# Decode attention's index tables moved to the top of the kernel

## The chip, the cores and the metric

The kernel runs on one core of a Trainium2 chip. The metric is device time in microseconds (us) of one execution. Before the change, three runs took 1286.26, 1288.38 and 1287.98 us; the median is 1287.98 us.

A core has five engines with a queue each: PE (TensorE, matrix products and transposes), DVE (VectorE), ACT (ScalarE), POOL (GpSimd) and SP, which here only issues transfers. Each works through its queue in order and waits on semaphores set by the others. Transfers are issued by SP, ACT or POOL and are carried out by 16 DMA engines.

## The reference

One inference step of a two-layer decoder trunk on 512 new prompt tokens and on 8 decode sequences of 4 new tokens each, all in float32, with a model width of 1024. Layer 0 mixes tokens with a convolution module, layer 1 with stick-breaking attention (16 heads of 64), and each is followed by a gated feed-forward network with a short convolution (ConvFFN, width 2816). The decode sequences attend to 256 past tokens, which lie in a paged pool of 128-token pages:

```python
k_past = [jnp.take(cache_k[a], page_table, axis=0).reshape(db, past_len, N_HEADS, HEAD_DIM) ...]
z = jnp.einsum('bqhd,bkhd->bhqk', q, k) * (HEAD_DIM ** -0.5)
z = z + bias[None, :, None, None]
log_fail = jnp.where(valid, jax.nn.log_sigmoid(-z), 0.0)
after = lax.cumsum(log_fail, axis=3, reverse=True) - log_fail
weights = jnp.where(valid, jnp.exp(jax.nn.log_sigmoid(z) + after), 0.0)
```

`page_table` (8 sequences by 2 pages, int32) says which page of the pool holds which part of a sequence. `bias` is one learned number per head, and `valid` is the causal mask.

## The kernel before

Activations are kept transposed, 128 features on the partitions and 544 tokens (512 prompt, 32 decode) along the row, in eight blocks: xT is the residual stream, XH and XL are its normalised value split into a high and a low part. Each weight block (`raw`, 1 MB, two buffers) is loaded by `Ring.load` (L338), cast to a high part by ACT (L375, `whi`) and subtracted to a low part by DVE (L378, `wlo`). Every product is three matrix multiplications. The first twelve blocks (`CONV_RAWS`) are loaded through POOL's queue, except for the very first, which are loaded in halves on SP's (L349); the rest go through SP's.

The work is written as lists. A `Plan` takes operations with an engine, an estimated cost in us and the keys that they read and write. `Plan.run` simulates the engines and fixes the order in which operations are emitted: on each engine it takes the ready operation with the earliest start, less a small share of its rank (the longest chain of work behind it). Within a list the order on each engine stays as planned; operations that are emitted outside a list are mixed in by the compiler's own scheduler. There is one list for the convolution, one for each layer's ConvFFN (the function `ffn`) and one for the attention. The list of the first ConvFFN, here the first layer's list, also holds the query products of layer 1 (`queries`), and at its end the first steps of the decode attention.

Those steps are three. First, xT is saved to memory (L1801), for the space of xT is wanted for pages: `page_t` is three buffers of 128 tokens by 1024 over the front of xT. Second, `decode_tables` makes the small tables in thirteen pieces, each entered in the list as a DVE operation of 0.5 us that comes after `ready`, the point at which the second half's normalisation may begin. Third, `gather` (L1940) fetches the first three pages of K rows on POOL's queue, with row numbers from the table `idx`; they come after the save and after the tables. The remaining 13 K gathers and 16 V gathers belong to the attention's list and reuse the same buffers.

The tables are: `idx`, for each partition and page the row number in the pool (page number times 128 plus the partition); `bcol`, the head's bias on each partition; `mnew`, the mask among the new tokens; and `own`, which partition belongs to which sequence. They come from two counting patterns of POOL (`iota`, L1948 and L1950), from `page_table` broadcast to all partitions (L1952) and from the biases `bb`, likewise broadcast (L1750).

Between the two lists stand operations that belong to none: Qz (in xT) and Qf are cleared (L2016, L2017), queries of the decode tokens are copied into them on POOL (L2026, L2032), and ACT's function table is changed. The attention's list then begins with the key products (L2108 to L2110), which also serve as filling, and with `page_logits`: PE transposes one page in two halves into the single PSUM buffer `t` (L2216), DVE copies out the first half and ACT the second (L2220), and then logits are computed (L2228).

At the top of the kernel SP loads the first prompt rows and weights, while POOL clears a few tiles and issues 23 small loads of parameters (`prow`, L627 to L633, and `trow`, L638) ahead of its first weight block. DVE has little to do before the first rows of x arrive (L943).

Of the kernel before, what the change touches and what calls it, by code (L numbers as in the profile page):

```python
# [21 lines left out]
NB = 8  # L22
NI = 4
NS = NB * NI
# [5 lines left out]
H = 16  # L30
HD = 64
EPS = 1e-6
NEG = -1.0e30
# [9 lines left out]
MORE = 3  # L43
CONV_RAWS = 12
PLAINQ = 4
TABLES = 13

PASSES = ((0, 4), (4, 6), (10, 6), (16, 6))
FFN_CHUNKS = 6
# [178 lines left out]
def tile_trunk(  # L228
# [8 lines left out]
    nc = tc.nc  # L237
# [11 lines left out]
    def close(cm):  # L249
        cm.__exit__(None, None, None)  # L250
# [155 lines left out]
    xT = base.tile([P, NC, T], F32, name="xT")  # L406
    XH = base.tile([P, NC, T], F32R, name="XH")
    XL = base.tile([P, NC, T], F32R, name="XL")
    NPRM = 42
    prm = base.tile([P, NC, NPRM], F32, name="prm")  # L410
    fprm = base.tile([P, NF, 40], F32, name="fprm")
# [197 lines left out]
    trow = [start.tile([8 * n_g, P], F32, name=f"trow{i}") for i in range(2)]  # L609
    zero = conv.tile([P, 2 * P], BF16, name="zero")  # L610
    dve.memset(zero, 0.0)
    act.dma_start(out=mrow[2:4, :], in_=conv_b_in.rearrange("o (t d) -> (o t) d", t=2))
    act_table("sqrt_and_others")
    nc.sync.dma_start(out=mrow[0:2, :], in_=norm_mix)
# [19 lines left out]
    for i in range(2):  # L634
        ch0 = (PE_CHUNKS[0] + i * len(PE_CHUNKS) // 2) * P
        for m in range(8):
            nj = min(4, CW - 4 * m)
            pool.dma_start(out=trow[i][m * n_g:(m + 1) * n_g, :nj * 32].rearrange("g (j h) -> g j h", j=nj),  # L638
                          in_=conv_w_dw[0, 4 * m:4 * m + nj, ch0:ch0 + n_g * 32].rearrange("j (g h) -> g j h", h=32))


    plan = Plan(E_CONV, 0.12)
# [580 lines left out]
    def ffn(l, before, after):  # L1223
# [455 lines left out]
        def queries(s):  # L1679
# [61 lines left out]
            def kept():  # L1741
                close(pools["more_cm"])
                close(cm)
                att["qk_cm"], qk = open_pool("qk")
                att["qT"] = qk.tile([P, NC, T], F32, name="qT")
                att["kT"] = qk.tile([P, NC, T], F32, name="kT")
                att["bb"] = qk.tile([P, H], F32, name="bb")
                att["kT_s"] = qk.tile([P, NC, NS], F32, name="kT_s")
                att["dz_cm"], att["dz"] = open_pool("dz")
                nc.sync.dma_start(out=att["bb"], in_=attn_b_logit[0].partition_broadcast(P))  # L1750

            ready = plan.op("none", 0.0, kept, after=range(opened, len(plan.ops)))

# [45 lines left out]
                s += 4  # L1799
            xs = [("x", c, h) for c in range(NC) for h in range(2)]  # L1800
            plan.op("sp", 5.0, lambda: nc.sync.dma_start(out=xsave, in_=xflat), r=[*xs, "normed1"], w=["saved"])  # L1801
            tables = decode_tables()
            for _ in range(TABLES):
                plan.op("dve", 0.5, lambda: next(tables), w=["tables"], after=[ready])
            for j in range(PAGE_BUFS):
                plan.op("pool", 1.05, lambda j=j: gather(page_t[j], j, ck), r=["saved", "tables"])
            return s
# [32 lines left out]
        after = after()  # L1840
# [97 lines left out]

    def gather(t, j, src):
        pool.indirect_dma_start(out=t, out_offset=None, in_=src,  # L1940
                                in_offset=bass.IndirectOffsetOnAxis(ap=att["idx"][:, j:j + 1], axis=0))

    def decode_tables():
        dz = att["dz"]
        bb = att["bb"]
        small_cm, small = open_pool("dsmall")
        pid = small.tile([P, 1], I32, name="pid")
        pool.iota(pid, pattern=[[0, 1]], base=0, channel_multiplier=1)  # L1948
        t32 = small.tile([P, NS], I32, name="t32")
        pool.iota(t32, pattern=[[1, NS]], base=0, channel_multiplier=0)  # L1950
        pt_i = small.tile([P, 2 * NB], I32, name="pt_i")
        nc.sync.dma_start(out=pt_i, in_=page_table.rearrange("b g -> (b g)").partition_broadcast(P))  # L1952
        ti = small.tile([P, 8], I32, name="ti")
        tf = small.tile([P, 8], F32, name="tf")
        dve.tensor_scalar(ti[:, 0:1], pid, 3, 3, op0=ALU.logical_shift_right, op1=ALU.bitwise_and)
        dve.tensor_scalar(ti[:, 1:2], pid, 3, None, op0=ALU.bitwise_and)
        dve.tensor_scalar(ti[:, 2:3], pid, 5, None, op0=ALU.logical_shift_right)
        yield 0.45
        dve.tensor_scalar(ti[:, 3:4], pid, 2, 1, op0=ALU.logical_shift_right, op1=ALU.bitwise_and)
        dve.tensor_copy(ti[:, 4:5], pid)  # L1960
        dve.tensor_copy(tf[:, 0:5], ti[:, 0:5])
        yield 0.45
        dve.scalar_tensor_tensor(tf[:, 5:6], tf[:, 2:3], 2.0, tf[:, 3:4], op0=ALU.mult, op1=ALU.add)
        cb_i = small.tile([P, 2, NS], I32, name="cb_i")
        dve.tensor_scalar(cb_i[:, 0, :], t32, 2, None, op0=ALU.logical_shift_right)
        dve.tensor_scalar(cb_i[:, 1, :], t32, 3, None, op0=ALU.bitwise_and)
        yield 0.45
        cb = small.tile([P, 2, NS], F32, name="cb")
        dve.tensor_copy(cb, cb_i)
        t32f = small.tile([P, NS], F32, name="t32f")  # L1970
        dve.tensor_copy(t32f, t32)
        mnew = dz.tile([P, 2, NS], F32, name="mnew")
        bcol = dz.tile([P, 2], F32, name="bcol")
        own = dz.tile([P, 4], F32, name="own")
        for b in range(4):
            dve.tensor_scalar(own[:, b:b + 1], tf[:, 0:1], float(b), None, op0=ALU.is_equal)
            yield 0.45
        m1 = small.tile([P, NS], F32, name="m1")
        for bg in range(2):
            rb = small.tile([P, 1], F32, name=f"rb{bg}")  # L1980
            dve.tensor_scalar(rb, tf[:, 0:1], float(4 * bg), None, op0=ALU.add)
            dve.tensor_scalar(m1, cb[:, 0, :], rb[:, 0:1], None, op0=ALU.is_equal)
            dve.scalar_tensor_tensor(mnew[:, bg, :], cb[:, 1, :], tf[:, 1:2], m1, op0=ALU.is_lt, op1=ALU.mult)
            yield 0.45
            dve.tensor_scalar(mnew[:, bg, :], mnew[:, bg, :], 1.0, -NEG, op0=ALU.subtract, op1=ALU.mult)
            rh = small.tile([P, 1], F32, name=f"rh{bg}")
            dve.tensor_scalar(rh, tf[:, 5:6], float(8 * bg), None, op0=ALU.add)
            oh = small.tile([P, H], F32, name=f"oh{bg}")
            dve.scalar_tensor_tensor(oh, t32f[:, :H], rh[:, 0:1], bb, op0=ALU.is_equal, op1=ALU.mult)
            yield 0.45  # L1990
            dve.tensor_reduce(bcol[:, bg:bg + 1], oh, axis=mybir.AxisListType.X, op=ALU.add)
        pt_f = small.tile([P, 2 * NB], F32, name="pt_f")
        dve.tensor_copy(pt_f, pt_i)
        dve.tensor_scalar(pt_f, pt_f, float(P), tf[:, 4:5], op0=ALU.mult, op1=ALU.add)
        yield 0.45
        idx = dz.tile([P, 2 * NB], I32, name="idx")
        dve.tensor_copy(idx, pt_f)
        close(small_cm)
        att.update(mnew=mnew, bcol=bcol, own=own, idx=idx)
        yield 0.1  # L2000

    ffn(0, nrm, None)
    mnew, bcol, own = (att[k] for k in ("mnew", "bcol", "own"))
    qT, kT, bb, kT_s, dz = (att[k] for k in ("qT", "kT", "bb", "kT_s", "dz"))
    wT = xflat[:, 3 * D:4 * D].rearrange("p (t g r) -> p t g r", t=4, g=2)

    KW = 2 * P
# [535 lines left out]
```

## Time and profile before

| what | value |
|---|---|
| median of 3 runs | 1287.98 us (1286.26 to 1288.38) |
| the profiled execution | 1286.75 us |
| its span | 1285.0 us |
| PE busy | 1265.0 us, 98% of the span |
| DVE busy | 1002.3 us, 78% |
| ACT busy | 717.8 us, 56% |
| POOL busy | 155.3 us, 12% |
| mean granted PE clock | 0.996 |

The span runs from the first to the last instruction that the profiler recorded; the execution's own time is 1.75 us longer. Times inside the profile count from the start of the span. Rows of the order of time begin with start and length in us; what follows in square brackets is how long the engine was idle before and what released it. A row may merge several instructions (x2, x4).

The lists lie as follows: the convolution from the start to about 219 us, the first ConvFFN and the queries of layer 1 from there to about 638 us, then the attention.

### The profile page before, as it was taken

How to read it: one execution, taken by the hardware profiler on the slowest of the kernel's cores; microseconds unless marked ns; L12 is line 12 of the kernel's file. 1: busy time of each engine (PE TensorE's matmuls, PEld its weight loads, DVE VectorE, ACT ScalarE, POOL GpSimd, SP SyncE). 2: the span in 40 equal slices, each digit the busy share in tenths (PEclk: the TensorE clock that was granted, in tenths of full speed). 3: DMA queues.
4: the chain of work that ended last, by engine and by line, in shares of the span. 5: the costliest groups of instructions: out<-in, count | busy, mean ns of one | idle time of the engine just before them, and what ended most of it. 6: DMA issues, size and time to landing. Idle time of an engine off the chain costs nothing. (4 is left out here: it accounts for less than half of the span.)

```text
span 1285.0 us, 26466 instructions
## 1 busy us (share of the span) xinstructions
PE 1265.0 (98%) x10836; PEld 1213.6 (94%) x10836; DVE 1002.3 (78%) x1699; ACT 717.8 (56%) x1436; POOL 155.3 (12%) x289
## 2 busy tenths in 40 slices
PE   9999999999999999999899999999999999999997
PEld 8997799999999999999888888899999999999997
DVE  6899876988987887769947577666988987886864
ACT  7596574645644445445547587654645555454453
POOL 4000014101001000000122223100111011000000
PEclk9999999999999999999989999999999999999999
DMA  7465233123232233143364544333132333232221
GB/s 226 123 175 139 85 100 114 34 89 110 91 115 93 89 95 116 60 140 137 100 212 123 166 148 162 107 116 99 50 100 87 96 117 115 67 109 93 88 77 70
DMA packets 119404, 142.39 MB, mean 111 GB/s; under 512 B 5358, under 2 KB 110470, under 8 KB 119011
## 3 DMA queue, kind: packets, MB, share of 16 engines
q1 hardware_dynamic: 110638, 111.91, 28.1%
q0 software_dynamic: 8640, 28.78, 7.0%
q8 instruction: 85, 1.39, 0.5%
q14 instruction: 37, 0.30, 0.1%
q10 hardware_dynamic: 4, 0.01, 0.0%
HBM read 129.34 MB, written 12.18 MB: 110 GB/s over the span
## 5 line engine op out<-in xcount | busy, mean ns | idle before, releaser
L375 ACT CAST whi<-raw 128x1024 fp32r<-128x1024 f32 (+2 forms) x247 | 224.5, 912 | 120.4 <-PE av L1324 25.7
L378 DVE TENSOR_TENSOR wlo<-raw,whi 128x1024 fp32r<-128x1024 f32 (+2 forms) x247 | 258.4, 1048 | 27.9 <-ACT whi L375 26.3
L677 PE MATMUL acc<-XH,whi 128*128 128x288 f32 (+1 forms) x384 | 114.5, 298 | 0.0
L678 PE MATMUL acc<-XL,whi 128*128 128x288 f32 (+1 forms) x384 | 110.9, 289 | 0.1
L679 PE MATMUL acc<-XH,wlo 128*128 128x288 f32 (+1 forms) x384 | 110.4, 288 | 0.1
L1323 PE MATMUL av<-HH,whi 128*128 128x288 f32 (+1 forms) x280 | 83.1, 297 | 0.2
L2108 PE MATMUL acc<-XH,whi 128*128 128x256 f32 (+1 forms) x264 | 83.3, 315 | 0.0
L1547 PE MATMUL acc<-TH,whi 128*128 128x272 f32 x288 | 82.9, 288 | 0.0
L1549 PE MATMUL acc<-TH,wlo 128*128 128x272 f32 x288 | 82.8, 288 | 0.0
L1548 PE MATMUL acc<-TL,whi 128*128 128x272 f32 x288 | 82.8, 287 | 0.0
L1324 PE MATMUL av<-HL,whi 128*128 128x288 f32 (+1 forms) x280 | 82.4, 294 | 0.0
L1325 PE MATMUL av<-HH,wlo 128*128 128x288 f32 (+1 forms) x280 | 82.2, 294 | 0.0
L1583 ACT COPY G<-acc 128x272 f32<-128x272 f32 (+1 forms) x72 | 26.8, 372 | 95.0 <-PE acc L1549 95.0
L1323 PE MATMUL tr<-HH,whi 128*128 128x256 f32 (+1 forms) x280 | 79.0, 282 | 0.0
L1324 PE MATMUL tr<-HL,whi 128*128 128x256 f32 (+1 forms) x280 | 78.9, 282 | 0.0
L1325 PE MATMUL tr<-HH,wlo 128*128 128x256 f32 (+1 forms) x280 | 78.4, 280 | 0.0
L2109 PE MATMUL acc<-XL,whi 128*128 128x256 f32 (+1 forms) x264 | 76.9, 291 | 0.0
L2110 PE MATMUL acc<-XH,wlo 128*128 128x256 f32 (+1 forms) x264 | 76.7, 290 | 0.0
L677 PEld LDWEIGHTS acc<-XH,whi 128*128 128x128 f32 x384 | 72.2, 188 | 2.8 <-issue 1.6
L678 PEld LDWEIGHTS acc<-XL,whi 128*128 128x128 f32 x384 | 72.3, 188 | 1.0 <-DVE XL L929 0.3
L679 PEld LDWEIGHTS acc<-XH,wlo 128*128 128x128 f32 x384 | 72.2, 188 | 0.3 <-DVE wlo L378 0.3
L1486 DVE SCALAR_TENSOR_TENSOR cv<-G,fprm,cv 128x560 f32<-128x560 f32 x88 | 69.3, 795 | 0.5
(456 smaller groups left out, 4367.0 us busy)
## 6 DMA issues: line engine op xcount, KB each, us to landing
raw<-in_ffn_w_gate_dram SPq DMA_DIRECT2D x22, 1024.0 KB
raw<-in_ffn_w_up_dram SPq DMA_DIRECT2D x22, 1024.0 KB, 5.2
raw<-in_ffn_w_down_dram SPq DMA_DIRECT2D x24, 768.0 KB, 4.7
raw<-in_attn_w_qkv_dram SPq DMA_DIRECT2D x12, 1024.0 KB, 6.2
raw<-in_conv_w_in_dram POOLq DMA_DIRECT2D x6, 1024.0 KB, 6.3
rep<-glu SPq DMA_DIRECT2D x36, 142.0 KB, 4.1
raw<-in_conv_w_out_dram POOLq DMA_DIRECT2D x4, 1024.0 KB, 6.5
raw<-in_ffn_w_down_dram SPq DMA_DIRECT2D x8, 512.0 KB, 3.4
```

The lines of the kernel that those rows point to most:

```text
L375: act.copy(hi[:, k, :], src[:, k])
L378: dve.tensor_tensor(lo[:, k, :], src[:, k], hi[:, k, :], op=ALU.subtract)
L677: pe.matmul(o, hi[:, k, :], XH[:, k, c0:c0 + n], start=(k == 0), stop=False)
L678: pe.matmul(o, hi[:, k, :], XL[:, k, c0:c0 + n], start=False, stop=False)
L679: pe.matmul(o, lo[:, k, :], XH[:, k, c0:c0 + n], start=False, stop=(k == NC - 1))
L1323: pe.matmul(o, hi[:, j + k, :], xh, start=(start and k == 0), stop=False, **kw)
L1324: pe.matmul(o, hi[:, j + k, :], xl, start=False, stop=False, **kw)
L1325: pe.matmul(o, lo[:, j + k, :], xh, start=False, stop=(stop and k == len(xs) - 1), **kw)
L1547: pe.matmul(o, hi[:, j + k, :], xh, start=(start and k == 0), stop=False, **kw)
L1548: pe.matmul(o, hi[:, j + k, :], xl, start=False, stop=False, **kw)
L1549: pe.matmul(o, lo[:, j + k, :], xh, start=False, stop=(k == 3), **kw)
L2108: pe.matmul(o, hi[:, k, :], XH[:, k, c0:c0 + n], start=(k == 0), stop=False)
```

## The change

The tables are split in four. `decode_tables` runs at the top of the kernel, outside any list, and makes what depends on no input: the two counting patterns, `own`, and the helpers `tf`, `cb`, `t32f` and `rb`. Their tiles are kept for the whole kernel (`base`, about 1.1 KB on each partition); the integer ones are in the start's pool. The loads of the page table and of the biases move from SP's queue, at the end of the first layer's list, to the end of POOL's row of small loads at the top. The page table is loaded straight into `idx`.

`decode_columns` (page numbers to row numbers, biases to columns) and `decode_masks` become one DVE operation each in the first layer's list, with estimates of 0.6 and 0.7 us. Neither has an operation to wait for in the list. The gathers still come after the save and after `tables`, which `decode_columns` now writes. The two heads' groups share one reduction, so that there are 31 DVE instructions in place of 32.

```diff
-TABLES = 13
@@
+    bb = base.tile([P, H], F32, name="bb")
+    mnew = base.tile([P, 2, NS], F32, name="mnew")
+    bcol = base.tile([P, 2], F32, name="bcol")
+    own = base.tile([P, 4], F32, name="own")
+    idx = base.tile([P, 2 * NB], I32, name="idx")
+    pt_f = base.tile([P, 2 * NB], F32, name="pt_f")
...
+    def decode_tables():
+        pid = start.tile([P, 1], I32, name="pid")
+        pool.iota(pid, pattern=[[0, 1]], base=0, channel_multiplier=1)
+        t32 = start.tile([P, NS], I32, name="t32")
+        pool.iota(t32, pattern=[[1, NS]], base=0, channel_multiplier=0)
...
+        for b in range(4):
+            dve.tensor_scalar(own[:, b:b + 1], tf[:, 0:1], float(b), None, op0=ALU.is_equal)
+        for bg in range(2):
+            dve.tensor_scalar(rb[:, bg:bg + 1], tf[:, 0:1], float(4 * bg), None, op0=ALU.add)
+            dve.tensor_scalar(tf[:, 6 + bg:7 + bg], tf[:, 5:6], float(8 * bg), None, op0=ALU.add)
+
+    def decode_masks():
+        for bg in range(2):
+            dve.tensor_scalar(m1, cb[:, 0, :], rb[:, bg:bg + 1], None, op0=ALU.is_equal)
+            dve.scalar_tensor_tensor(mnew[:, bg, :], cb[:, 1, :], tf[:, 1:2], m1, op0=ALU.is_lt, op1=ALU.mult)
+            dve.tensor_scalar(mnew[:, bg, :], mnew[:, bg, :], 1.0, -NEG, op0=ALU.subtract, op1=ALU.mult)
+
+    def decode_columns():
+        for bg in range(2):
+            dve.scalar_tensor_tensor(oh[:, bg, :], t32f[:, :H], tf[:, 6 + bg:7 + bg], bb, op0=ALU.is_equal, op1=ALU.mult)
+        dve.tensor_reduce(bcol, oh, axis=mybir.AxisListType.X, op=ALU.add)
+        dve.tensor_copy(pt_f, idx)
+        dve.tensor_scalar(pt_f, pt_f, float(P), tf[:, 4:5], op0=ALU.mult, op1=ALU.add)
+        dve.tensor_copy(idx, pt_f)
+
+    decode_tables()
@@
+    pool.dma_start(out=idx, in_=page_table.rearrange("b g -> (b g)").partition_broadcast(P))
+    pool.dma_start(out=bb, in_=attn_b_logit[0].partition_broadcast(P))
@@
-                att["bb"] = qk.tile([P, H], F32, name="bb")
...
-                nc.sync.dma_start(out=att["bb"], in_=attn_b_logit[0].partition_broadcast(P))
@@
-            tables = decode_tables()
-            for _ in range(TABLES):
-                plan.op("dve", 0.5, lambda: next(tables), w=["tables"], after=[ready])
+            plan.op("dve", 0.6, decode_columns, w=["tables"])
+            plan.op("dve", 0.7, decode_masks)
             for j in range(PAGE_BUFS):
                 plan.op("pool", 1.05, lambda j=j: gather(page_t[j], j, ck), r=["saved", "tables"])
@@
-                                in_offset=bass.IndirectOffsetOnAxis(ap=att["idx"][:, j:j + 1], axis=0))
...
+                                in_offset=bass.IndirectOffsetOnAxis(ap=idx[:, j:j + 1], axis=0))
```

The old `decode_tables`, a generator of thirteen pieces with its own pool of tiles, is removed.

More of the change, by code (lines that the diff above doesn't have):

```diff
@@ L408, in tile_trunk @@
     XL = base.tile([P, NC, T], F32R, name="XL")
+    bb = base.tile([P, H], F32, name="bb")
[4 more added lines that the diff above has]
+    pt_f = base.tile([P, 2 * NB], F32, name="pt_f")
+    tf = base.tile([P, 8], F32, name="tf")
+    t32f = base.tile([P, NS], F32, name="t32f")
+    oh = base.tile([P, 2, H], F32, name="oh")
+    cb = base.tile([P, 2, NS], F32, name="cb")
+    m1 = base.tile([P, NS], F32, name="m1")
+    rb = base.tile([P, 2], F32, name="rb")
     NPRM = 42
@@ L611, in tile_trunk @@
     dve.memset(zero, 0.0)
+    def decode_tables():
[3 more added lines that the diff above has]
+        pool.iota(t32, pattern=[[1, NS]], base=0, channel_multiplier=0)
+        ti = start.tile([P, 8], I32, name="ti")
+        cb_i = start.tile([P, 2, NS], I32, name="cb_i")
+        dve.tensor_scalar(ti[:, 0:1], pid, 3, 3, op0=ALU.logical_shift_right, op1=ALU.bitwise_and)
+        dve.tensor_scalar(ti[:, 1:2], pid, 3, None, op0=ALU.bitwise_and)
+        dve.tensor_scalar(ti[:, 2:3], pid, 5, None, op0=ALU.logical_shift_right)
+        dve.tensor_scalar(ti[:, 3:4], pid, 2, 1, op0=ALU.logical_shift_right, op1=ALU.bitwise_and)
+        dve.tensor_copy(ti[:, 4:5], pid)
+        dve.tensor_copy(tf[:, 0:5], ti[:, 0:5])
+        dve.scalar_tensor_tensor(tf[:, 5:6], tf[:, 2:3], 2.0, tf[:, 3:4], op0=ALU.mult, op1=ALU.add)
+        dve.tensor_scalar(cb_i[:, 0, :], t32, 2, None, op0=ALU.logical_shift_right)
+        dve.tensor_scalar(cb_i[:, 1, :], t32, 3, None, op0=ALU.bitwise_and)
+        dve.tensor_copy(cb, cb_i)
+        dve.tensor_copy(t32f, t32)
+        for b in range(4):
[3 more added lines that the diff above has]
+            dve.tensor_scalar(tf[:, 6 + bg:7 + bg], tf[:, 5:6], float(8 * bg), None, op0=ALU.add)
@@ L1940, in gather @@
         pool.indirect_dma_start(out=t, out_offset=None, in_=src,
-                                in_offset=bass.IndirectOffsetOnAxis(ap=att["idx"][:, j:j + 1], axis=0))
[L1943 to L2000, printed above, removed]
@@ L2002, in tile_trunk @@
+                                in_offset=bass.IndirectOffsetOnAxis(ap=idx[:, j:j + 1], axis=0))
     ffn(0, nrm, None)
-    mnew, bcol, own = (att[k] for k in ("mnew", "bcol", "own"))
-    qT, kT, bb, kT_s, dz = (att[k] for k in ("qT", "kT", "bb", "kT_s", "dz"))
+    qT, kT, kT_s, dz = (att[k] for k in ("qT", "kT", "kT_s", "dz"))
     wT = xflat[:, 3 * D:4 * D].rearrange("p (t g r) -> p t g r", t=4, g=2)
```

## The prediction

> **What bounds the kernel now.** I read four views: the share of each engine, TensorE's (PE's) waits, two-microsecond windows of the longest wait, and the order of time on each engine around it.
>
> ```profile
> PE 1265.0 (98%) x10836; PEld 1213.6 (94%) x10836; DVE 1002.3 (78%) x1699; ACT 717.8 (56%) x1436; POOL 155.3 (12%) x289
> ...
> PE t L2216 <- DMA xT<-in_cache_k_dram,idx: 5.8, 1, 5.8
> ...
> PE tr L847 <- DVE ysum L831: 1.3, 1, 1.3
> ...
> PE av L1547 <- ACT qT L1789: 0.5, 1, 0.5
> ```
>
> PE is busy for 98% of the span, so time is won only where PE stands still or runs slowly. One wait is four times as long as any other: the transposes of the first cache page (L2216) wait 5.8 us for the first gather of K rows.
>
> ```profile
> 638.33 0.28 PE L2108 MATMUL acc<-XH,whi 128*128 128x256 f32 x1
> ...
> 638.93 0.28 PE L2110 MATMUL acc<-XH,wlo 128*128 128x256 f32 x1
> 645.00 1.12 PE L2216 MATMUL t<-ident,xT 128*128 128x128 f32 x4 [5.79 <-DMA xT<-in_cache_k_dram,idx]
> ...
> 646.13 0.41 PE L2109 MATMUL acc<-XL,whi 128*128 128x256 f32 x1
> 646.34 0.41 PE L2110 MATMUL acc<-XH,wlo 128*128 128x256 f32 x1
> ...
> 648.48 1.05 PE L2216 MATMUL t<-ident,xT 128*128 128x128 f32 x4
> ...
> 650.61 0.36 PE L2108 MATMUL acc<-XH,whi 128*128 128x288 f32 x1
> ...
> 134.00:136.00 2.00, 1.10 (x7) 1.05 (x8) 0.79 (x3) 0.39 (x2) 0.00 (x0) 1.00 0.03 8
> ...
> 642.00:644.00 2.00, 0.00 (x0) 0.00 (x0) 0.00 (x0) 0.00 (x0) 1.70 (x2) 0.97 0.79 213
> 644.00:646.00 2.00, 1.00 (x5) 1.00 (x6) 0.00 (x0) 0.00 (x0) 0.57 (x2) 0.50 1.05 376
> 650.00:652.00 2.00, 2.00 (x15) 2.00 (x15) 0.00 (x0) 0.53 (x2) 0.75 (x1) 0.82 0.23 39
> ```
>
> (The window rows give busy time of PE, weight load, DVE, ACT, POOL, then the granted clock.) The wait has a second price. During it the clock falls to 0.50, and the matmuls that follow start 0.21 us apart (646.13 to 646.34) instead of 0.12 us (five steps from 638.33 to 638.93) until 650.61. The shorter wait of 1.3 us at 134 us left the clock at 1.00.
>
> Why is the page late? These are POOL's and DVE's rows just before:
>
> ```profile
> 602.36 1.18 POOL L2016 MEMSET xT<- 128x1280 f32 x1 [12.44 <-DVE qT L1671]
> 637.56 0.62 POOL L2026 COPY xT<-qT 64x128 f32<-64x128 f32 x2 [34.02 <-DVE pt_f L1993]
> 638.24 1.29 POOL L2032 COPY Qf<-qT 64x128 f32<-64x128 f32 x4
> 639.81 1.71 POOL L1940 DMA_INDIRECT xT<-in_cache_k_dram,idx  x1 [0.29 <-POOL Qf L2032]
> ...
> 637.91 0.30 DVE L1997 CAST idx<-pt_f 128x16 int32<-128x16 f32 x1
> 638.54 0.44 DVE L1791 SCALAR_TENSOR_TENSOR qT<-av,qT 128x272 f32<-128x272 f32 x1 [0.33 <-PE av L1549]
> 639.29 2.44 DVE L378 TENSOR_TENSOR wlo<-raw,whi 128x1024 fp32r<-128x1024 f32 x2 [0.31 <-ACT whi L375]
> 646.15 0.69 DVE L2220 COPY kT<-t 128x512 f32<-128x512 f32 x1 [4.42 <-PE t L2216]
> ```
>
> The indices are ready at 638.21. The gather stands in POOL's queue behind the query copies (L2026, L2032), which end at 639.53, and its data take until 645.00. The space it writes was free far earlier: L2016 clears part of the same xT at 602.36, and what it waited for was the last read of xT by the norm (L1671). So from 602.4 on only the index chain held the pages back.
>
> **The change, part by part.** *Gathers, the gain.* With idx made near the list's start, a gather waits only for the save of xT and its last readers, which the memset's row puts at 602.4. Three gathers, each holding POOL for 1.7 us at most and landing within 9 us of issue, are there by about 616, 23 us before PE asks; the DMA engines are idle in that stretch (0.00 in the window row's share). In POOL's queue the gathers then stand beside the memset and ahead of the query copies; these wait for queries until 637.56 anyway.
>
> ```profile
> DMA to landing us min/median/max: 4.0/5.0/8.6
> ...
> 600.00:620.00 20.00, 20.00 (x157) 20.00 (x157) 19.90 (x36) 12.19 (x23) 1.18 (x1) 1.00 0.00 1
> ```
>
> (The first row is of all 32 gathers, from issue to landing.)
>
> PE thus goes on at 639.21 (638.93 + 0.28): 5.79 us saved. Its half-speed stretch goes too: from 645.00 to 650.61 are 5.61 us; at the ratio 0.12/0.21 = 0.57 it would take 3.2, and at exactly half 2.8, so 2.4 to 2.8 us more, of which I take 2.6. Sum of the gain: 8.4 us.
>
> [...]
>
> *What is late next.* The buffer t is single. The second half of page 0 can be transposed only when DVE has copied the first half (L2220), and in DVE's queue that copy stands behind the two L378 of 639.29, which wait for ACT's casts:
>
> ```profile
> 638.21 1.99 ACT L375 CAST whi<-raw 128x1024 fp32r<-128x1024 f32 x2 [0.77 <-DVE idx L1997]
> 640.22 1.28 ACT L447 ACT_TABLE_LOAD   x1
> ```
>
> Their end, 641.7, does not depend on the tables: the cast begins when its raw block lands. The copy then runs to 642.4, and PE may go on near 642.5. PE gets there after four transposes (0.4) and twelve matmuls of 0.12: 639.21 + 1.85 = 641.1. So a new wait of 1.4 us; bounds 0 (copy or subtractions come earlier) and 1.5. Like the wait at 134 us it is too short to cost the clock. ACT's table load ends at 641.5, before its first copy is due. Net at this place: 8.4 - 1.4 = 7.0 us.
>
> *DVE work out of the tail.* Thirteen listed pieces leave the list's end. Their 32 instructions lie between 594 and 638 us, among DVE work that keeps it busy for 19.9 of 20 us, but PE waits there only once, 0.5 us for a query evacuation (L1547). I value this at 0, bounds -0.5 (that wait goes) and +0.5 (another such one comes). Their two loads, of the page table and of bb, leave SP's queue; no PE wait hangs on what follows them there.
>
> *Columns and masks at the start of the first layer's list.* They have no predecessor in the list, so they come first on DVE.
>
> ```profile
> 219.84 0.07 DVE L1466 MEMSET G<- 128x2 f32 x2
> 226.07 1.95 DVE L1354 RECIPROCAL rstd<-rstd 128x288 f32<-128x288 f32 x1 [6.16 <-ACT rstd L1351]
> ```
>
> Here DVE is idle for 6.2 us. Six instructions for the columns and six for the masks, at the 0.2 to 0.3 us that such rows take (L1997 above), are about 2.7 us: hidden. Without this cover they would put off the reciprocal, and with it the normalised second half, by 2.7 us.
>
> *Tables at the top.* Nineteen small DVE instructions, and on POOL two iotas of about 0.14 us. In the old tail nine such instructions started within 0.8 us, so some 2 us in all.
>
> ```profile
> 4.90 1.23 DVE L943 SCALAR_TENSOR_TENSOR ext_s<-xr 128x1024 f32<-128x1024 f32 x1 [3.01 <-DMA xr<-in_x_prompt_dram]
> 594.14 0.14 DVE L1955 TENSOR_SCALAR ti<-pid 128x1 int32<-128x1 int32 x1
> ...
> 594.93 0.17 DVE L1966 TENSOR_SCALAR cb_i<-t 128x32 int32<-128x32 int32 x1
> ...
> 589.20 0.14 POOL L1948 IOTA pid<- 128x1 int32 x1 [32.51 <-DVE XL L1674]
> ```
>
> DVE waits 3 us for the first block of x there, so they cost nothing.
>
> *Two more loads in POOL's queue.* idx and bb are issued after the sixteen loads of trow and before the third weight block:
>
> ```profile
> 18.46 0.56 POOL L638 DMA_DIRECT2D trow<-in_conv_w_dw_dram  x1 [0.51 <-DMA trow<-in_conv_w_dw_dram]
> 19.57 0.94 POOL L338 DMA_DIRECT2D raw<-in_conv_w_in_dram  x1 [0.56 <-DVE va L714]
> ...
> DMA to landing us min/median/max: 6.3/6.3/6.3
> ...
> 25.90 1.05 ACT L375 CAST whi<-raw 128x1024 fp32r<-128x1024 f32 x1
> ...
> 28.55 0.51 DVE L929 SCALAR_TENSOR_TENSOR XL<-tr,prm,XH 128x288 fp32r<-128x288 f32 x1
> ...
> 29.24 0.40 PE L677 MATMUL acc<-XH,whi 128*128 128x288 f32 x1
> ...
> 31.92 0.46 DVE L960 COPY rstd<-tr 128x288 f32<-128x288 f32 x1 [0.77 <-PE tr L957]
> ```
>
> A small load holds POOL for 0.56 us and a large one for 0.94; no row shows a broadcast of 128 short rows. Two cost 1.1 to 1.9 us; nearest is the small load, plus the queue's short waits: 1.3 us. The block is issued at 19.57 and lands 6.3 us later, at 25.87, and ACT casts it at 25.90: no slack. So the cast comes at 27.2, and ACT's and DVE's conversions of x behind it come later too. PE uses those at 29.24, just after DVE's 28.55 + 0.51. But not all of the lateness need reach PE: DVE idles for 0.8 us before 31.92, where it catches up that much. Bounds 0 and 1.9 us; of 1.3 less 0.8 I take 0.4, as PE's products of 29.24 need not be the ones that use the late columns.
>
> **Sum.** -5.8 - 2.6 + 1.4 + 0.4 = -6.6 us. The profiled execution took 1286.75 us, so it becomes 1280.15. The median of the runs shown is 1.2 us above it; carrying most of that, I forecast 1281.0 us.
>
> **Rivals.** *The gathers stay where they are in POOL's queue.* They are listed within the layer, but the final order mixes in the query copies, and before it put these first. If they remain ahead, the first gather starts at 639.53 instead of 639.81 and only 0.3 us is won, less the 0.4 at the top: 1288, no change. Against it: L2016 shows that work on xT is let through at 602, and the gather is older in the program. Chance 0.10.
>
> *The whole gain.* The list is rebuilt without 6.5 us of planned DVE time; if the two subtractions or the copy come earlier, the wait of 1.4 us is not there: 1279.6. Chance 0.14.
>
> *A dearer start.* The third block's 1.9 us go through to PE and the new wait grows by one subtraction (1.2 us): 1281.0 + 1.5 + 1.2 = 1283.7. Chance 0.12. [...]
>
> *Slower: the tail's new order.* From 600 to 620 us DVE is idle for 0.1 us of 20. The planner gave the tables 6.5 us there, and they took half; without them it sorts subtractions (1.2 us each in the pair at 639.29) against the query evacuations anew. Each subtraction that slips ahead of an evacuation PE needs costs up to 1.2 us. Six cancel the gain; eight give 1281 + 9.6 = 1290.6. Against it: the tables were small and low in rank, and most subtractions are tied to casts and loads. Chance 0.05.
>
> **How the numbers follow.** Likeliest is the sum, 0.59; its own range is 1279 to 1283. The range of 1278.0 to 1286.0 takes in the whole gain and the dearer start, and leaves out no change, slower, and thin tails. A difference of 0.2% (2.6 us) is about what can be told from none. Faster: 0.59 + 0.14 + 0.12 = 0.85; same 0.10; slower 0.05.
>
> **What would show it.** Right: gathers L1940 start near 602 to 606 us; no PE wait on a K gather; clock 1.00 from 638 to 652; a wait of 1 to 1.5 us at the second L2216 with DVE's copy as its releaser; columns inside DVE's gap before the reciprocal; the third raw block issued about 1.3 us later. The prediction is wrong if the gathers still follow L2032, if PE waits elsewhere in 600 to 660, or if PE shows idle time near 29 us above 1 us.

## The result, and the profile after

The changed kernel takes 1277.03 us (median of 6 runs, 1276.49 to 1277.93), the kernel before 1286.78 us (6 runs, 1286.21 to 1288.38). The ratio is 0.9923, with a 95% interval of 0.991 to 0.9936: 0.8% faster. The forecast was 1281.0 us with a range of 1278.0 to 1286.0; the direction was right, and the time came out 1 us below the range. The profiled execution took 1276.92 us, 9.83 us less than the one before (1286.75 us).

The line numbers of the changed kernel differ: L2216 is now L2206, L2220 is L2210, L1940 is L1990, L378 is L377, L375 is L374, L2016 is L2006, L2026 and L2032 are L2016 and L2022, L1354 is L1407, L338 is L337.

First the share of each engine and PE's waits, in the changed kernel (us in total, times, longest).

```profile
PE 1259.6 (99%) x10836; PEld 1207.7 (95%) x10836; DVE 1001.6 (79%) x1698; ACT 718.5 (56%) x1436; POOL 161.0 (13%) x291
...
PE t L2206 <- DVE kT L2210: 0.9, 1, 0.9
...
PE tr L1010 <- DVE XL L982: 0.5, 1, 0.5
```

The wait of 5.8 us for the K gather has gone from the list. The two small ones shown are new. Next the order of time on POOL, PE and DVE around the place.

```profile
598.87 1.51 POOL L1990 DMA_INDIRECT xT<-in_cache_k_dram,idx  x1 [9.94 <-ACT XH L1726]
...
602.21 2.84 POOL L1990 DMA_INDIRECT xT<-in_cache_k_dram,idx  x1 [0.30 <-ACT XH L1726]
605.05 1.18 POOL L2006 MEMSET xT<- 128x1280 f32 x1
636.62 0.63 POOL L2016 COPY xT<-qT 64x128 f32<-64x128 f32 x2 [30.38 <-ACT qT L1840]
637.31 3.25 POOL L2022 COPY Qf<-qT 64x128 f32<-64x128 f32 x4
...
638.10 0.60 PE L2206 MATMUL t<-ident,xT 128*128 128x128 f32 x4
641.05 0.66 PE L2206 MATMUL t<-ident,xT 128*128 128x128 f32 x4 [0.94 <-DVE kT L2210]
...
637.95 2.44 DVE L377 TENSOR_TENSOR wlo<-raw,whi 128x1024 fp32r<-128x1024 f32 x2
640.32 0.68 DVE L2210 COPY kT<-t 128x512 f32<-128x512 f32 x1
```

Two windows of the same kernel (length, then PE, weight load, DVE, ACT and POOL busy, then the granted clock):

```profile
640.00:642.00 2.00, 1.06 (x9) 0.95 (x9) 1.00 (x2) 0.28 (x2) 1.09 (x3) 1.00 0.26 47
642.00:644.00 2.00, 2.00 (x19) 2.00 (x18) 0.31 (x1) 0.71 (x2) 0.96 (x1) 1.00 1.00 341
```

The three gathers stand at 599 to 605 us, ahead of the memset and 30 us ahead of the query copies. PE goes from its last matmul straight into the first transposes at 638.10, waits 0.94 us at the second for DVE's copy, which stands behind the two subtractions, and keeps full clock.

The subtractions begin earlier than before, and so does the load of the last weight block ahead of the page (SyncE's queue, first in the kernel before, then in the changed one):

```profile
633.00 0.37 SPq L338 DMA_DIRECT2D raw<-in_attn_w_qkv_dram  x1
```

```profile
631.59 0.37 SPq L337 DMA_DIRECT2D raw<-in_attn_w_qkv_dram  x1
```

In both it is issued as a subtraction of VectorE ends (at 632.97 and 631.57 us), and the cast of its block begins 5.2 and 5.1 us later (638.21 and 636.73).

The columns and masks and the start are as follows.

```profile
219.24 0.38 DVE L656 SCALAR_TENSOR_TENSOR oh<-t32f,tf,bb 128x16 f32<-128x16 f32 x2
...
221.53 0.18 DVE L652 TENSOR_SCALAR mnew<-mnew 128x32 f32<-128x32 f32 x1
...
225.45 1.95 DVE L1407 RECIPROCAL rstd<-rstd 128x288 f32<-128x288 f32 x1 [3.63 <-ACT rstd L1404]
...
1.23 0.15 DVE L631 TENSOR_SCALAR ti<-pid 128x1 int32<-128x1 int32 x1
...
2.84 0.14 DVE L646 TENSOR_SCALAR tf<-tf 128x1 f32<-128x1 f32 x1
...
2.09 0.73 POOL L678 DMA_DIRECT2D prow<-in_conv_w_dw_dram  x1
2.82 0.54 POOL L679 DMA_DIRECT2D prow<-in_conv_b_dw_dram  x1
...
19.91 0.60 POOL L691 DMA_DIRECT2D idx<-in_page_table_dram  x1
20.49 0.58 POOL L692 DMA_DIRECT2D bb<-in_attn_b_logit_dram  x1
21.05 1.82 POOL L337 DMA_DIRECT2D raw<-in_conv_w_in_dram  x2
...
31.00 1.04 PE L1010 MATMUL tr<-dg,mean_m 128*128 128x128 f32 x6 [0.47 <-DVE XL L982]
```

Columns and masks take 2.5 us (219.24 to 221.71) of a gap in which DVE stays idle for another 3.63 us. The tables take 1.75 us at the top. The third weight block is issued 1.48 us later than before (21.05 for 19.57), and PE waits 0.47 us near 31 us.

To see where the 9.8 us arise, the starts of the same matmul in both traces were subtracted (after less before, the median of 30 neighbours). The difference is +0.04 us at 45 us, -0.94 at 630, -8.43 at 680 and -9.46 at 1250; the rest, 0.4 us, lies behind PE's last matmul. So the page's place gave 7.5 us, and about 2 us came bit by bit, without any wait, in stretches which the change doesn't touch.

### The profile page after: what moved, and what is told of

It is laid out like the page before. It is cut to its first block, busy times and chain, and to the rows that moved or that the text cites. A ratio compares the mean times of both kernels' runs of the same rounds, so it can differ in the third digit from the quotient of the medians.

```text
span 1275.2 us, 26461 instructions
## 1 busy us (share of the span) xinstructions
PE 1259.6 (99%) x10836; PEld 1207.7 (95%) x10836; DVE 1001.6 (79%) x1698; ACT 718.5 (56%) x1436; POOL 161.0 (13%) x291
## 5 line engine op out<-in xcount | busy, mean ns | idle before, releaser
L374 ACT CAST whi<-raw 128x1024 fp32r<-128x1024 f32 (+2 forms) x247 | 224.4, 911 | 118.8 <-PE av L1377 25.1
L377 DVE TENSOR_TENSOR wlo<-raw,whi 128x1024 fp32r<-128x1024 f32 (+2 forms) x247 | 258.5, 1049 | 30.7 <-ACT whi L374 29.2
```

Of the source, the lines that this page charges most:

```text
L374: act.copy(hi[:, k, :], src[:, k])
L377: dve.tensor_tensor(lo[:, k, :], src[:, k], hi[:, k, :], op=ALU.subtract)
```

## The experiments

The reading so far leaves two questions: whether the early pages are the cause of the 7.5 us, and what the other 2 us are. Below, a "drift" is how much the difference of starts changes along a stretch in which PE doesn't wait.

### The changed kernel again, and the pages held back

The first run is the changed kernel, unedited.

> The changed kernel once more, unedited, as the measure for the other runs and as a second sample of its profile. Both theories: 1277.0 us, within 1 us, and 9 to 10.5 us below the kernel before. What it tells apart is the part of the gain that no step of the prediction names: from the start to 560 us the changed kernel won 0.6 to 0.8 us and after 660 us another 1. If that part belongs to the program, the second profile shows it at the same places; if it is variation between executions, it comes out anywhere between 0 and 2 us.

It took 1277.59 us (1276.35 to 1277.75), ratio 0.9918 (0.9905 to 0.9932). The second profile shows the same drift at the same places (-0.47 us from 45 to 120 us, -0.56 from 190 to 630, -0.89 from 805 to 940), so it belongs to the program.

In the second run the columns and the gathers come late again:

```diff
+ def evac():
+     if c2 == NC - 2 and what[0] == "21":
+         decode_columns()
+     dve.scalar_tensor_tensor(dst(), p()[:, :n], 0.125, dst(), ...)
...
- plan.op("dve", 0.6, decode_columns, w=["tables"])
+ plan.op("dve", 0.6, lambda: None, w=["tables"])
...
- plan.op("pool", 1.05, lambda j=j: gather(page_t[j], j, ck), r=["saved", "tables"])
+ plan.op("pool", 1.05, lambda: None, r=["saved", "tables"])
...
  # behind the list's run
+ for j in range(PAGE_BUFS if l == 0 else 0):
+     gather(page_t[j], j, ck)
```

> The changed kernel, but the columns (page numbers and biases) are made on VectorE only just before the last query evacuation of the first layer's list, and the first three gathers stand behind that list's run, so that they follow the query copies on GpSimd as before. Theory (the gain comes from the early gathers): the PE wait for the first gather of K rows is back at 5 to 6 us, the clock falls to 0.50 for some 5.6 us after it, and the second transpose's wait for VectorE's copy (0.94 us) is gone: 5.8 + 2.6 - 0.9 = 7.5 us over the changed kernel, 1284.5 us. Rival (the relief of VectorE's tail and the tables' removal from the list are worth the time, the gathers little): within 1.5 us of the changed kernel, 1277 to 1278.5 us.

It took 1287.34 us, ratio to before 1.0 (0.9991 to 1.0009), as long as the kernel before and 2.8 us longer than the theory's 1284.5. The order of time on POOL and PE in this kernel:

```profile
637.59 2.18 POOL L2028 COPY Qf<-qT 64x128 f32<-64x128 f32 x4
639.84 0.52 POOL L2067 MEMSET Zw<- 128x512 f32 x1
640.69 1.08 POOL L1996 DMA_INDIRECT xT<-in_cache_k_dram,idx  x1 [0.33 <-issue]
...
647.46 1.11 PE L2212 MATMUL t<-ident,xT 128*128 128x128 f32 x4 [8.89 <-DMA xT<-in_cache_k_dram,idx]
```

Windows of one microsecond of it, where the clock falls and where it comes back:

```profile
642.00:643.00 1.00, 0.00 (x0) 0.00 (x0) 0.00 (x0) 0.00 (x0) 0.92 (x1) 0.80 0.66 198
...
652.00:653.00 1.00, 1.00 (x7) 1.00 (x7) 0.00 (x0) 0.58 (x1) 0.74 (x1) 0.58 0.00 0
```

The gathers came out behind one more memset than in the kernel before, so the wait is 8.89 us and not 5 to 6. Between 620 and 660 us this kernel loses 10.35 us against the control: 8.89 for the wait, less 0.97 for the copy's wait that it no longer meets, and 2.4 us for the half clock. That it comes out level with the kernel before is partly chance: its wait is 3.1 us longer than the 5.79 us there, and against this it keeps the drift (-0.48, -0.54 and -0.90 us). What the run shows is the page's own part, which goes when the gathers are late again. The rival (VectorE's relief) falls: most of the tables are out of the list's tail here too, and the time is far from 1277 to 1278.5 us.

### The clock's part alone

Forty-five matmuls ahead of the first transposes keep PE busy while it waits, in the kernel before; their product isn't used.

```diff
  def turn(t=t, pt=pt, half=half, first=n == pg == half == 0):
+     for _ in range(45 if first else 0):
+         pe.matmul(pt()[:, :2 * P], XH[:, 0, :P], XH[:, 0, :2 * P], start=True, stop=True)
```

> The kernel before, with 45 matmuls of 256 columns ahead of the first page's transposes, whose product nobody reads, so that PE works on while it waits for the gather (45 x 0.12 = 5.4 us at full clock, within the wait of 5.8 us). It prices the clock's part alone. Theory (half clock costs 2.6 us, bounds 2.4 to 2.8): clock 1.00 over the whole stretch, the gather's landing unchanged, and 2.4 to 2.8 us less than the kernel before, some 1284.2 us; less 0.9 to 1.4 us of it if then the second transpose has to wait for VectorE's copy. [...]

The order of time on PE in this kernel:

```profile
640.50 0.28 PE L2110 MATMUL acc<-XH,wlo 128*128 128x256 f32 x1
640.62 5.55 PE L2215 MATMUL t<-XH 128*128 128x256 f32 x45
646.63 0.66 PE L2218 MATMUL t<-ident,xT 128*128 128x128 f32 x4 [0.46 <-DMA xT<-in_cache_k_dram,idx]
...
650.35 0.29 PE L2110 MATMUL acc<-XH,wlo 128*128 128x288 f32 x1
650.98 0.63 PE L2218 MATMUL t<-ident,xT 128*128 128x128 f32 x4 [0.34 <-DMA xT<-in_cache_k_dram,idx]
```

The last product ahead of the second page in the kernel before:

```profile
651.34 0.29 PE L2110 MATMUL acc<-XH,wlo 128*128 128x288 f32 x1
```

The window in which PE goes on, with the matmuls added:

```profile
646.00:648.00 2.00, 1.54 (x14) 1.38 (x13) 0.68 (x1) 0.00 (x0) 0.19 (x1) 1.00 1.08 380
```

The clock stays at 1.00, and the gather lands as late as before: the first page's transposes start 6.13 us after the start of the last product (640.50 to 646.63), against 6.07 us in the kernel before (638.93 to 645.00). From the last product ahead of the first page to the last one ahead of the second, PE takes 12.41 us in the kernel before (638.93 to 651.34) and 9.85 us here (640.50 to 650.35): 2.56 us for the clock. That lies within the forecast (2.4 to 2.8). PE then meets a new wait of 0.34 us for the second gather, so that 2.0 us are left at 660 us. The median, 1286.47 us, ratio 0.999 (0.9981 to 0.9999), agrees with a gain but is too wide to size it.

### The two microseconds without a wait: the place of the tiles

The new tables are declared in the lasting part of SBUF (`base`), behind xT, XH and XL and ahead of the later tiles. The twelve tiles have 1,152 bytes a partition as declared; with each rounded up to 32 bytes, which is the author's assumption, they take 1,216. No trace shows the addresses or the rounding, but the drifts below fit 1,216 (-0.47 us from 45 to 120 us, like 64 and 192 bytes) and not 1,152, a multiple of 128 (0.00 to +0.20 us at 128, 512 and 1,024). In the kernel before, the same twelve are added, and nothing else.

```diff
+ pads = [base.tile(s, d, name=f"pad{i}") for i, (s, d) in enumerate((
+     ([P, H], F32), ([P, 2, NS], F32), ([P, 2], F32), ([P, 4], F32), ([P, 2 * NB], I32), ([P, 2 * NB], F32),
+     ([P, 8], F32), ([P, NS], F32), ([P, 2, H], F32), ([P, 2, NS], F32), ([P, NS], F32), ([P, 2], F32)))]
...
+ for t in pads:
+     dve.memset(t, 0.0)
```

> The kernel before, with twelve more small tiles in the lasting part of SBUF, of the same sizes as those that the change adds there, cleared once at the top; all later tiles lie as far along in SBUF as in the changed kernel, and nothing else is altered. Theory of displacement (the 2 us that no step of the prediction names come from where the tiles lie, since matmuls of 256 columns start 1 to 2 per cent closer together after the change): 1 to 2 us less than the kernel before. Rival (those 2 us are variation between executions, or follow from the order of work): within 0.5 us of the kernel before.

> The padded kernel (twelve tiles of 1,152 bytes in SBUF, nothing else) once more, since its median lay 4.1 us under the kernel before while its profile showed 1.9 us less. If the place of the tiles is worth 2 us and the rest was chance (the first 40 us of single executions differ by up to 2 us), the median comes out at 1284.5 to 1286 us, and the profile shows the same drift of PE's starts, -0.8 us between 40 and 640 us and -1.1 us between 640 and 940 us. If the place is worth 4 us, the median is 1283.4 us again and the second profile shows where the other 2 us lie.

The first run gave 1283.39 us, ratio 0.9968 (0.9956 to 0.998), the second 1284.25 us, 0.9975 (0.9965 to 0.9985). Both profiles drift as the changed kernel does. Four more sizes were added to the kernel before, as one tile in place of the list of twelve, and one to the changed kernel:

```diff
+ pads = [base.tile([P, 32], F32, name="pad0")]      # 128 bytes; [P, 128]: 512; [P, 48]: 192; [P, 16]: 64
+ pad0 = base.tile([P, 32], F32, name="pad0")        # the changed kernel: 1,216 + 128 = 1,344 bytes
```

> The kernel before, with one tile of 32 floats (128 bytes a partition) more in the lasting part of SBUF, cleared once at the top, where the padded kernel had twelve tiles of 1,152 bytes together. Theory of place (what counts is where a tile lies, not how much lies before it): PE's starts drift from those of the kernel before by another amount, of either sign, between -2 and +1 us by 960 us. Rival (the drift grows with the bytes added): 0.2 us or less.

> The kernel before with 128 floats (512 bytes a partition) more in the lasting part of SBUF, cleared once at the top. By 940 us PE's starts drifted by -1.9 us with 1,152 bytes and by +0.9 us with 128 bytes. Theory of place: again another drift, of either sign. Rival (the drift depends on the sum of the bytes by a straight line through the two points): about 0 us, within 0.3 us.

> The changed kernel with 32 floats (128 bytes a partition) more in the lasting part of SBUF, behind the new tables, cleared once at the top. Theory of place (128 bytes ahead of the later tiles cost the kernel before 0.6 us by 940 us whatever lies before them): PE's starts drift by some +0.3 to +1 us from those of the changed kernel. Rival (each place has its own drift, which can't be told beforehand): anything from -1 to +2 us. A drift within 0.1 us would speak against both.

> The kernel before with one tile of 48 floats (192 bytes a partition) more in the lasting part of SBUF, cleared once at the top: the remainder of 1,216 to 512 bytes. Theory of the remainder: the same drift of PE's starts as with the twelve tiles, -0.8 us between 40 and 640 us and -1.1 us between 640 and 940 us. Rival (the twelve tiles' drift comes from 1,216 bytes as such): another drift, or none.

> The kernel before with one tile of 16 floats (64 bytes a partition) more in the lasting part of SBUF, cleared once at the top. The changed kernel with 128 bytes more stands at 1,344 bytes, which leaves 64 by 256 and 320 by 512, and drifted like the changed kernel, to within 0.3 us. If the remainder to 256 bytes decides, 64 bytes drift like it: about -1.7 us by 940 us. If the remainder to 512 decides, 64 bytes are a place not seen yet, between 0 and 128 bytes: -0.3 to +0.9 us.

Finally the change without its shift: two tiles share space with others, so that 1,024 bytes are added by the same count, and each engine runs its instructions in the changed kernel's order.

```diff
- pt_f = base.tile([P, 2 * NB], F32, name="pt_f")
...
+ pt_f = t32f[:, :2 * NB]
...
- m1 = base.tile([P, NS], F32, name="m1")
+ m1 = oh.rearrange("p g h -> p (g h)")
```

> The changed kernel in its own order of instructions on every engine, but two of the new tiles lie in others (the page numbers' tile in the counting row's, the masks' scratch row in the biases' one-hot tile), so that 192 bytes a partition are saved: what is added ahead of the later tiles is 1,024 instead of 1,216 bytes, a whole multiple of the 512 bytes with which the kernel before showed no drift. It is the change without its shift of place. Theory (the pitch follows the place by its remainder to 512 bytes): PE's starts go along with those of the kernel before up to 638 us within 0.2 us, and come out later than those of the changed kernel by 0.8 us between 40 and 640 us and by 1.1 us between 640 and 940 us; the median is 1279.2 us, which is what the prediction's own terms would have to be held against. Rival (the pitch follows the bytes in another way, or the new tiles themselves): within 0.3 us of the changed kernel's starts, 1277.3 us.

The drift of PE's starts against the kernel before, in us, worked out from the traces as above:

```
bytes added  kernel                  45-120 us  190-630 us  805-940 us  median us, ratio (95% interval)
 512         before + one tile          0.00      +0.06       +0.02     1287.11  1.0002 (0.9992-1.0012)
1024         the change, tiles shared   0.00       0.00       +0.05     1279.34  0.9941 (0.9927-0.9954)
 128         before + one tile         +0.20      -0.12       +0.23     1288.19  1.0007 (0.9997-1.0017)
  64         before + one tile         -0.46      -0.32       -0.83     1287.53  0.9997 (0.9986-1.0007)
 192         before + one tile         -0.47      -0.50       -0.92     1284.60  0.9977 (0.9967-0.9987)
1216         before + twelve tiles     -0.47      -0.47       -0.90     1283.39  0.9968 (0.9956-0.998)
1216         the same again            -0.47      -0.36       -0.91     1284.25  0.9975 (0.9965-0.9985)
1216         the change                -0.47      -0.48       -0.90     1277.03  0.9923 (0.991-0.9936)
1344         the change + one tile     -0.47      -0.31       -0.83     1276.64  0.9917 (0.9899-0.9935)
```

The rows behind it are of this kind. The last transpose of the attention's output and the first mean of the norm after it, first in the kernel before and then in the change with shared tiles (1,024 bytes), the changed kernel and the kernel before with 192 bytes:

```profile
850.60 0.44 PE L2315 MATMUL one<-ident,oacc 128*128 128x128 f32 x2
...
904.13 0.65 PE L1349 MATMUL tr<-sqa,mean_m 128*128 128x288 f32 x2
```

```profile
845.08 0.44 PE L2305 MATMUL one<-ident,oacc 128*128 128x128 f32 x2
...
898.61 0.65 PE L1402 MATMUL tr<-sqa,mean_m 128*128 128x288 f32 x2
```

```profile
841.94 0.44 PE L2305 MATMUL one<-ident,oacc 128*128 128x128 f32 x2
...
894.96 0.65 PE L1402 MATMUL tr<-sqa,mean_m 128*128 128x288 f32 x2
```

```profile
850.45 0.44 PE L2318 MATMUL one<-ident,oacc 128*128 128x128 f32 x2
...
903.45 0.65 PE L1352 MATMUL tr<-sqa,mean_m 128*128 128x288 f32 x2
```

The distance is 53.53, 53.53, 53.02 and 53.00 us. PE never waits for more than 0.6 us at a time in the three stretches, before and after the change; its matmuls simply start closer together, by less than 1 ns each on the mean (in the changed kernel 0.48 us over 765 of them, 0.48 over 3,479 and 0.90 over 1,189). It is not all of them: from 190 to 630 us the whole 0.48 us lies in the steps behind the 1,084 products of high weights with the activations' low part, 0.4 ns each. From all nine rows of the table follows: where the bytes added leave 64 when divided by 128 (64, 192, 1,216, 1,344), PE wins about 0.5, 0.4 and 0.9 us in the three stretches; where they are a multiple of 128 (128, 512, 1,024), it wins nothing, and 128 bytes lose a little. The remainder to 512, which an expectation had put first, is not what decides: 64 and 1,344 bytes leave different ones and drift alike. The smaller differences (128 bytes against 512 and 1,024; 64 and 1,344 against 192 and 1,216) would fit the remainder to 256, on few rows. Two expectations missed: 512 bytes gave the rival's nothing, though a straight line through the other points does not hold either, and 128 bytes behind the new tables cost 0.2 us by the three stretches where 0.3 to 1 was expected. How the place acts on PE was not tried.

The change without this shift takes 1279.34 us (1279.18 to 1280.57), as expected of the theory (1279.2). That is what moving the tables is worth by itself, 0.6%; the other 0.2% come from where the later tiles happen to lie. The two ratios' intervals just overlap (0.9927 to 0.9954 and 0.991 to 0.9936); the drifts, the same in every profile, are what tells the two kernels apart. What the time of single padded runs adds stays open in part: with twelve tiles the median fell by 3.2 and 4.1 us where the drift gives 2, and with 64 bytes it did not fall though the drift is there. The profile of the second padded run has a shorter page wait (4.93 us), that of 64 bytes a longer one (8.6 us). How late the page is differs from run to run, which would hide the drift in kernels that wait for it; that was not separated.

### Three tries at what is left

The second half of page 0 into another PSUM buffer:

```diff
- pt = psum("t")
+ pt = psum("av" if n == pg == 0 and half else "t")
```

> The changed kernel, but the second half of page 0 is transposed into a PSUM buffer of the attention's products instead of the buffer t, so that it need not wait for VectorE's copy of the first half. Theory (the new wait of 0.94 us before the second transpose is the single buffer's, and the rest of the list is indifferent): that wait is gone, and the time falls by 0.9 us to some 1276.4 us. Rival (the wait only moves: VectorE's copies stay as late as they are, and PE meets the next of them instead): PE waits about 0.9 us a few matmuls later, and the time stays at 1277.3 us.

It took 1277.42 us, ratio 0.992 (0.9906 to 0.9933), the same as the changed kernel. The order of time on PE shows why:

```profile
640.38 0.60 PE L2206 MATMUL av<-ident,xT 128*128 128x128 f32 x4
642.89 0.66 PE L2206 MATMUL t<-ident,xT 128*128 128x128 f32 x4 [1.21 <-DVE kT L2210]
```

The second half goes without a wait, and the first half of page 1, which needs t again, waits 1.21 us. The wait belongs to DVE's late copy and not to the number of buffers; the rival held.

So the copy was given to another engine. ScalarE copies the first half of page 0, VectorE the second (the copy below it takes engine and cost from `eng`):

```diff
- eng = ("dve", "act")[half]
+ eng = ("dve", "act")[half ^ (n == pg == 0)]
...
```

> The changed kernel, but of page 0 ScalarE copies the first half out of the buffer t and VectorE the second (the other way round for this page alone). VectorE's copy stands behind two subtractions of together 2.44 us that end at 640.4 us; ScalarE is through with its casts and its table load at 640.03 us and needs 0.59 us. Theory (the wait of 0.94 us is the copy's place in VectorE's queue): PE waits 0.5 us instead of 0.94 us, 0.4 us won, some 1276.9 us. Rival (it only moves, as in the run with the other buffer): 1277.3 us.

The order of time on ACT and PE in this kernel:

```profile
639.27 1.28 ACT L458 ACT_TABLE_LOAD   x1
640.57 0.59 ACT L2210 COPY kT<-t 128x512 f32<-128x512 f32 x1
...
641.21 0.66 PE L2206 MATMUL t<-ident,xT 128*128 128x128 f32 x4 [0.60 <-ACT kT L2210]
```

The wait falls to 0.60 us, and PE gains 0.33 us there (0.4 was expected). The median, 1277.17 us, ratio 0.9921 (0.9907 to 0.9934), can't tell that from nothing.

The two small loads on SyncE's queue:

```diff
+ nc.sync.dma_start(out=idx, in_=page_table.rearrange("b g -> (b g)").partition_broadcast(P))
+ nc.sync.dma_start(out=bb, in_=attn_b_logit[0].partition_broadcast(P))
- pool.dma_start(out=idx, in_=page_table.rearrange("b g -> (b g)").partition_broadcast(P))
- pool.dma_start(out=bb, in_=attn_b_logit[0].partition_broadcast(P))
```

> The changed kernel, but the page table and the logit biases are loaded on SyncE's queue behind the first loads of x instead of on GpSimd's. Theory (the two loads cost the third weight block 1.2 to 1.5 us in GpSimd's queue, of which PE feels the wait of 0.47 us near 31 us): the block is issued at 19.6 to 19.9 us instead of 21.05, that wait goes, and 0.5 us are won: 1276.8 us. Rival (PE has slack there and the wait only moves to the next piece): no change, 1277.3 us, or worse by up to 0.6 us where the two loads put back SyncE's next loads.

It took 1278.17 us, ratio 0.9928 (0.9914 to 0.9941). On POOL:

```profile
20.62 0.56 POOL L691 DMA_DIRECT2D trow<-in_conv_w_dw_dram  x1 [0.59 <-DMA trow<-in_conv_w_dw_dram]
21.28 1.84 POOL L337 DMA_DIRECT2D raw<-in_conv_w_in_dram  x2
```

The weight block is issued at 21.28 us, no earlier than behind the two loads (21.05): the last rows of trow now wait longer for earlier ones to land. The theory falls, and nothing was won: PE's wait of 0.47 us isn't in this profile, but it isn't in the control's either. Both edits together (another buffer, SyncE's queue):

> The two edits before this one together: the second half of page 0 in another PSUM buffer, and the two small loads on SyncE's queue. Theory (both waits are real and apart, 600 us from each other): the gains add, 1.4 us less than the changed kernel, 1275.9 us. Rival (either wait only moves): 1276.5 to 1277.3 us.

1278.16 us, ratio 0.9927 (0.9913 to 0.994): no gain either, though the weight block is issued at 20.64 us, and the wait for DVE's copy is 1.72 us there. No version tried is measurably better than the changed kernel.

## Where the prediction was right, and where it wasn't

**The gather and what it blocks: right.** The gathers start at 598.87 to 602.21, against 602 to 606 foretold, and one holds POOL for 2.84 us, against 1.7 at most; with 30 us in hand neither matters. PE meets the page at 638.10 without a wait; late pages, put back with a wait of 8.89 us, cost 10.35 us between 620 and 660. The rival in which the gathers stay behind the query copies is excluded by the rows.

**The price of the half clock: right.** 2.6 us were taken from the ratio of two pitches; 2.56 us were measured with PE kept busy, and 2.4 with the pages held back. How long the clock stayed low in each run (3.42, 6.82 or 10.24 us) stands in the last section.

**The wait that takes its place: right in kind, mis-sized.** 1.4 us foretold, 0.94 measured, with DVE's copy as its releaser and the two subtractions in front of it. They end at 640.39 us, 2.3 us after PE reaches the page; the prediction had 641.7 against 639.21, 2.5 us. They were taken to stand still, not to depend on the tables, but they moved 1.3 us (the row of 639.29 became 637.95): the first of them works on a block whose load follows VectorE's own queue, and this load is issued 1.4 us earlier. PE came 0.95 us earlier itself (638.93 became 637.98); the other 0.4 to 0.5 us fit VectorE's tail without the tables, which no run took apart. PE also took 2.0 us to the second transpose (638.10 to 640.12), not 1.85. The net at this place is 7.5 us instead of 7.0.

**VectorE's work out of the tail: right.** It was valued at 0, and PE's wait for a query evacuation is still there with 0.5 us. Neither slower order nor further waits came.

**Two more loads: right in the queue, without effect on the sum.** The block is issued 1.48 us later (1.3 foretold), the cast begins at 27.78 us (27.2 foretold), and PE waits 0.47 us (0.4 foretold). But PE had started 0.4 us earlier in this execution, where its 19 warm-up matmuls at the top took 3.83 us instead of 4.24, so that it was no later than before at 45 us (+0.04). That is luck, and not the slack that the prediction argued with. In the control, where PE is 1.2 us later, that wait isn't there. In other words the cost hangs on how early PE comes there in that run.

**Columns, masks, tables at the top: right.** Hidden in DVE's gap (2.5 us, with 3.63 us of it left over) and ahead of x. POOL's first two loads begin at 2.09 and 2.82 us, while the tables run on DVE (1.23 to 2.98 us), and take 0.73 and 0.54 us, as before (0.72 and 0.55).

**The step that failed: the tables' tiles were costed as instructions only.** Under "Tables at the top" the prediction counts nineteen instructions and two iotas, and ends with "they cost nothing". That the tiles are kept for the whole kernel, and so push 1,216 bytes, by the count above, along in front of the others, got no term and no bound. It is worth 2.0 us (1279.34 less 1277.03 is 2.3 by the medians, 1.8 to 2.0 by the drift), and without it the time would have come out inside the range. Of the 3.2 us between the sum (-6.6) and the profile (-9.8), 2.0 are this drift, and the rest is 0.5 for the page's place, 0.4 for the head and 0.4 behind PE's last matmul. This last part lies between the issue of the output's stores and the end (5.0 us, 5.3 before); the control has it too (5.0), and the padded kernel hasn't (5.4), so it belongs to the changed program. Why, no run shows. The last 0.8 us of the 4 are the carried difference of the median: 1.2 us from three runs, while 22 later runs of the kernel before have their median at 1287.49, 0.7 us above the profiled execution, and the changed kernel's profiled execution lies at its median.

With the place taken out, the kernel at 1,024 bytes (1279.34 us) is within the likeliest case's own range of 1279 to 1283.

## What to carry to other kernels

Where a gather waits for small index work at the end of a list, making the indices early is worth the wait and the slow clock behind it (here 5.79 and 2.6 us), less what waits next (0.94 us), and the next wait is found by asking what the first freed instruction needs from each engine's queue. When a change adds or removes tiles that outlive a stage, compare the matmul starts stretch by stretch before crediting the edit: an even drift in stretches without waits can be the place of the tiles (here about 2 us), and a pad of the same size on the old kernel separates the two. Here a wait on a late copy (0.94 us) wasn't cured with a second buffer (1.21 us half a page later); an earlier copy made it shorter (0.60 us).

## What the runs showed of the hardware that was not expected

**The half clock lasted 3.42 us, or two or three times that.** Windows of one microsecond of the kernel before (the same columns as above):

```profile
643.00:644.00 1.00, 0.00 (x0) 0.00 (x0) 0.00 (x0) 0.00 (x0) 0.89 (x1) 0.95 0.83 319
...
650.00:651.00 1.00, 1.00 (x7) 1.00 (x7) 0.00 (x0) 0.31 (x2) 0.75 (x1) 0.64 0.00 0
```

and of the second padded run:

```profile
644.00:645.00 1.00, 0.38 (x3) 0.38 (x4) 0.00 (x0) 0.00 (x0) 0.96 (x2) 0.94 0.54 99
645.00:646.00 1.00, 1.00 (x7) 1.00 (x6) 0.43 (x1) 0.00 (x0) 0.48 (x1) 0.50 0.95 290
...
648.00:649.00 1.00, 1.00 (x9) 1.00 (x8) 0.00 (x0) 0.28 (x1) 0.04 (x1) 0.85 1.12 411
```

The clock between is 0.50 in each. Taken that it is either 1.00 or 0.50, a window of one microsecond at clock c holds (1 - c) / 0.5 us of half clock. So the clock is low for 0.10 + 6 + 0.72 = 6.82 us in the first, 0.12 + 3 + 0.30 = 3.42 in the second, and 0.40 + 9 + 0.84 = 10.24 us in the kernel with the pages held back: within 0.02 us two, one and three times 3.42 us. Three more runs give the same lengths: 0.68 + 6 + 0.14 = 6.82 us in the same padded kernel's first run, 0.40 + 6 + 0.42 = 6.82 with 192 bytes and 0.82 + 9 + 0.42 = 10.24 with 64. What sets the length, no run shows. The cost comes from what is left of the low clock after PE resumes, 5.72 us (645.00 to 650.72) in the first. In the second all 3.42 us count: PE had resumed at 644.62, and the clock was low from 644.88 to 648.30. So it differs from run to run, in the same padded kernel too (6.82 and 3.42 us).

**64 bytes left over of 128 are worth 0.12 to 0.15% of the time** by PE's starts (1.6 to 1.9 of 1287 us in the six rows of 64, 192, 1,216 and 1,344 bytes), in stretches in which PE has no wait above 0.6 us before and after the change (the table above). Why, no run here shows.

**POOL's copies beside DVE's subtractions.** The four Qf copies take 3.25 us in the changed kernel (637.31), where the two subtractions run beside them (637.95 to 640.39), against 1.29 us before. With the pages held back they take 2.18 us (637.59). Nothing waits for them here. Whether the subtractions cause it, no run separated.
